# Shifting the stationary weight parts by 128 bytes in an fp32 decoder layer, and undividing the divided products

## The chip, the cores and the metric

One Trainium2 chip, one core. The metric is the device time of one execution of the kernel, in microseconds (us); the lower the better. TensorE (PE) multiplies; each of its products is a weight load (PEld: 128 columns of the operand that stands still, the stationary one) and a matmul that streams the other operand (the moving one) past it into PSUM. VectorE (DVE), ScalarE (ACT) and GpSimd (POOL) work element by element; SyncE (SP) issues the weight transfers.

## The reference

One decoder layer on 256 rows of width 2048, all in fp32:

```
h += 0.5 * post_norm(FFN1(rms_norm(h)))            SwiGLU, d_ff 5632
h += post_norm([conv_group ; moba_group] @ w_out)  one input projection, 5 x 1024 columns
h += post_norm(attn(rms_norm(h), rms_norm(mem)) @ w_o)   cross-attention, 4 heads, 256 memory rows
h += 0.5 * post_norm(FFN2(rms_norm(h)))
```

With 256 rows in one block, the block-sparse attention is plain causal attention with 8 heads of 128. The convolution has 31 taps and 1024 channels, and is followed by a layer norm and a swish.

## The kernel before, in words

**Products in three parts.** Every large product is made of TensorE products of type fp32r. Weights and activations are split into a high part (hi, an ACT copy) and a low part (lo, the rest, a DVE subtraction), and x times w is made as hi*hi + lo*hi + hi*lo: three products of 256 moving columns each, which write to the same place in PSUM.

**The weight stream (class `Weights`).** The weights arrive as entries of 128 x 1024 numbers in the order of use: SP loads an entry into one of 4 `raw` tiles, ACT writes its hi part into one of 4 `hi` tiles (L199 with a gain, L197 without), DVE its lo part into one of 3 `lo` tiles (L215, L213). `step` (L341) calls `W.ahead()`, which queues splits up to three entries ahead for hi and two for lo, then issues the 24 products of one entry, then one step of the background queue `bg`. Some entries are split early and kept in the general 8 KB buffers called `ck` (chunk): the activations, and of the weights those of the cross-attention's keys and of its output projection.

**Which operand stands still.** In `proj_T` (L485: both gate-up stages, the input projection's groups other than v, the cross-attention's q) the weight part is stationary and the activations' chunk moves. In `proj` (L499: both down stages, v, the two output projections) a chunk is stationary and the weight part moves. Each entry is 24 products: 16 with hi, 8 with lo. One gate-up is 22 groups of 8 entries (4,224 products), one down 88 entries (2,112).

**Where the tiles stand.** SBUF addresses are counted in bytes within a partition. In the program as built, the `hi` and `lo` tiles are 4096 bytes each and all start at 64 modulo 256; the chunks are 8192 bytes each and all start at 128 modulo 256. All slices that a product reads start a multiple of 512 bytes into their tile. Below, **the offset** of a product is the address of its stationary slice less that of its moving slice, modulo 256: 192 in the gate-ups and the input projection (64 - 128), 64 in the downs and in v (128 - 64), and 0 where chunk meets chunk, which is so in the cross-attention's keys (L485, `ps<-ck`) and its output projection (L499, `ps<-ck`).

**Divided products.** `HALVED = (0, 4, 8)` names three of the products of one entry (or of one half of it) which are issued as two matmuls of 128 columns instead of one of 256. That is done at 15 places, once each: in the first gate-up at (group, entry) (0, 2) and (3, 1); in the second at (1, 1) and (2, 1); in each of the three downs at entry 1 and entry 5 of the first column half; in groups 1 and 3 of the gated convolution and in the second group of q and k; and in both v groups.

**Interruptions.** Between these products TensorE makes small plain fp32 products, each of them two passes (two loads and two matmuls): the row-scale product at L447, `ones` times a diagonal, which spreads the rows' scales over the lanes (five times: in both gate-ups, in the second half of the first down, in the input projection and in the cross-attention's q), the attention's scores and values, the layer norm's sums (L993, L1009) and transposes (L362, L398).

**The stretch before the second gate-up.** After the attention weights' values (`x_values`) the split heads `oT` are stationary in the output projection. Before it, `W.ahead(2, 2)`, and after its first half `W.ahead()`, let ACT and DVE split the first entries of the second gate-up. Then come the post norm, the residual, transposes and splits of the new rows (L370 hi, L373 lo), and the gate-up starts.

Of the kernel before, what the change touches and what calls it, by code (L numbers as in the profile page):

```python
# [26 lines left out]
SCALE = 128.0 ** -0.5  # L27
RAW, HI, LO, TMP = 4, 4, 3, 4
STEP_DVE, STEP_ACT, STEP_POOL = 1.2, 1.3, 2.4
# [5 lines left out]
SIDE = 3  # L35
HALVED = (0, 4, 8)
MEM_AT = [20, 22, 24, 26]
# [63 lines left out]
class Weights:  # L101


    def __init__(self, nc, pool, chunk, sm):
        self.nc, self.pool, self.chunk, self.sm = nc, pool, chunk, sm
        self.entries = []
        self.raw, self.hi, self.lo, self.chunks = {}, {}, {}, {}
        self.n_raw = self.n_hi = self.n_lo = self.pos = 0
        self.marks = []
        self.limit = None  # L110

    def add(self, src, gains=(None,), key=None, rows=False):
        self.entries.append((src, gains, key, rows))

    def load(self, upto):
# [6 lines left out]
    def start(self):  # L122
# [12 lines left out]
        self.hi[key], self.lo[key] = ck[:, :, 0, :], ck[:, :, 1, :]  # L135
        self.hi[1] = self.pool.tile([P, 1024], F32R, name="hi", bufs=HI)
        self.lo[1] = self.pool.tile([P, 1024], F32R, name="lo", bufs=LO)

# [42 lines left out]
    def split_hi(self, upto):  # L181
        while self.n_hi < min(upto + 1, len(self.entries)):
            i = self.n_hi
            self.load(i)
            _, _, key, rows = self.entries[i]
            if rows:
                self.chunks[key] = c = self.chunk()
                self.hi[key], self.lo[key] = c[:, :, 0, :], c[:, :, 1, :]
            elif key is not None:
                c = self.chunk().rearrange("p a b c -> p (a b c)")  # L190
                self.hi[key], self.lo[key] = c[:, 0:1024], c[:, 1024:2048]
            else:
                key = i
                self.hi[key] = self.pool.tile([P, 1024], F32R, name="hi", bufs=HI)
            for src, dst, g in self.parts(i, self.hi[key]):
                if g is None:
                    self.nc.scalar.activation(dst, src, AF.Copy)  # L197
                else:
                    self.nc.scalar.activation(dst, src, AF.Copy, scale=g)  # L199
            self.n_hi += 1  # L200

    def split_lo(self, upto):
        while self.n_lo < min(upto + 1, len(self.entries)):
# [3 lines left out]
            if key is None:  # L207
                key = i
                self.lo[key] = self.pool.tile([P, 1024], F32R, name="lo", bufs=LO)
            his = self.parts(i, self.hi[key])  # L210
# [33 lines left out]
def layer_kernel(ctx: ExitStack, tc: tile.TileContext, x, mem, eye, consts, smalls, post_g, xt, memt,  # L244
# [51 lines left out]
    def add_ffn(gu, down, gain, extra, side):  # L296
        for n, (g, u) in enumerate(gu_order(side)):
            extra(-1, n)
            W.add(gu[g, u], [gain + 2 * u, gain + 2 * u + 1])
        for hf in range(2):  # L300
# [20 lines left out]
    for n in range(10):  # L321
        for u in range(8):
            W.add(w_in[n, u])
    for hf in range(2):
# [5 lines left out]
    for n in range(16):  # L330
        u = n % 8
        if n < 8:
            W.add(x_q[u], [S_GX + 2 * u, S_GX + 2 * u + 1])
        else:
            W.add(x_v[u // 4, u % 4])
# [153 lines left out]
    def proj(pss, first, last, hi, lo, xk, t, n0=0, halved=(), sides=(0, 256)):  # L489

        xs = [xk[:, f, t * P:(t + 1) * P] for f in (0, 1, 0)]
        m = 0
# [62 lines left out]

    def down(nk, lhs, post, hook=None, tail=TAIL, keep=False, order=None):

        order = order or range(nk)
        for hf in range(2):
# [3 lines left out]
            def mm(n, hi, lo):  # L563
# [3 lines left out]
                for t in range(2):  # L567
                    at = HALVED if t == 0 and (hf, n) in ((0, 1), (0, 5)) else ()
                    proj(pss[t], n == 0, n == nk - 1, hi, lo, lhs(order[n]), t, 0, at)
# [218 lines left out]
    post = Post(0, 4.0)  # L788
    last = down(KF, lambda k: hT[k // 4][:, k % 4], post, ffn1_hook)

# [61 lines left out]
    def glu_group(q):  # L852
        pss = in_group(halved=HALVED if q % 2 else ())
        box = []
# [222 lines left out]
    def v_group(c, hook):  # L1077
# [3 lines left out]
        def mm(u, hi, lo):  # L1081
            for e in range(2):
                k = 2 * u + e
                for t in range(2):
                    at = [m - 6 * t for m in HALVED] if u == 2 and e == 0 else ()
                    proj([vps[t]], k == 0, k == KT - 1, hi[:, e * 512:], lo[:, e * 512:], rows.x(k), t, 0, at)

# [14 lines left out]
    for c in range(2):  # L1102
        for p in range(2):
            pss = in_group(lambda u: norm_conv(c == 1 and p == 1 and u == 5), HALVED if (c, p) == (0, 1) else ())
            if p == 0:
# [99 lines left out]
    warm_sqrt()  # L1205
    oT = chunk()
    post = Post(2, 1.0)

    def x_values(hh):
        o_ = bank()  # L1210
        for t in range(2):
            nc.tensor.matmul(o_[:, :256], vx[:, hh // 2, t, (hh % 2) * P:(hh % 2 + 1) * P],  # L1212
                             pxT[:, hh * 512 + t * 256:hh * 512 + (t + 1) * 256], start=t == 0, stop=t == 1)
        make_hi(oT[:, hh, 0, :], o_[:, :256])
        make_lo(oT[:, hh, 1, :], o_[:, :256], oT[:, hh, 0, :])

    for hh in range(XH):
        x_values(hh)
    W.ahead(2, 2)
    wo = [W.held(("o", u)) for u in range(8)]  # L1220
    ps0 = [bank() for _ in range(4)]
    for hf in range(2):
        for k in range(XH):
            proj(ps0[2 * hf:2 * hf + 2], k == 0, k == XH - 1, *wo[4 * hf + k], oT[:, k], 0)
    W.ahead()
    rows = Rows(h_rows)
# [9 lines left out]
    for c in range(4):  # L1236
        ps1.append(bank())
        for sides in [(0, 256)] if c < 3 else [(0,), (256,)]:
            for k in range(XH):
                proj([ps1[c]], k == 0, k == XH - 1, *wo[4 * (c // 2) + k], oT[:, k], 1, c % 2, (), sides)  # L1240
    for c in range(4):
# [136 lines left out]
```

## Time and profile before

| | |
|---|---|
| median of 3 runs | 1901.75 us (1901.65 to 1904.34) |
| profiled execution | 1902.49 us, of which 1900.7 us span |
| TensorE busy | 1888.0 us, 99% of the span |
| TensorE's weight loads busy | 1883.2 us, 99% |
| VectorE, ScalarE, GpSimd busy | 62%, 55%, 11% |
| TensorE clock granted, mean | 0.999 of full |

TensorE is never idle for long, so the time is the number of products by the time from one product's start to the next one's, plus the short stops. A busy share of 99% says nothing about that pace; the starts of the weight loads do, and the rows below show them.

### The profile page before, as it was taken

The numbers are of one execution on the slowest core, as the hardware profiler recorded it, in microseconds if no ns is written. First come the engines' busy times: TensorE is split into PE (matmuls) and PEld (weight loads), VectorE is DVE, ScalarE is ACT, GpSimd is POOL, SyncE is SP. The second block draws the span as 40 slices with busy tenths as digits, with TensorE's granted clock in tenths as the row PEclk, the third lists the DMA queues.
The fourth block names the chain that finished last, engine by engine and source line by source line (L and its number), as shares of the span: only waits on it lengthen the run. The fifth ranks groups of instructions, "written<-read, shape, count | busy, mean of one in ns | idle before, by whom it ended". The sixth has DMA issues, their size and how long they took to land.

```text
span 1900.7 us, 39775 instructions
## 1 busy us (share of the span) xinstructions
PE 1888.0 (99%) x16445; PEld 1883.2 (99%) x16445; DVE 1179.5 (62%) x1615; ACT 1049.8 (55%) x1631; POOL 204.3 (11%) x182
## 2 busy tenths in 40 slices
PE   9999999999999999999999999999999999999998
PEld 9999999999999999999999999999999999999998
DVE  5666666666545556899885676666666666544444
ACT  6655555555434546687675565555555555433433
POOL 0000000000000000598510000000000000000000
PEclk9999999999999999999999999999999999999999
DMA  8555555555655675555555563565555555655554
GB/s 300 203 190 196 193 195 193 193 196 191 218 191 196 245 235 173 183 180 189 176 189 186 176 228 107 181 198 191 193 196 194 195 192 197 213 196 191 196 193 145
DMA packets 102278, 370.29 MB, mean 195 GB/s; under 512 B 11472, under 2 KB 11984, under 8 KB 101328
## 3 DMA queue, kind: packets, MB, share of 16 engines
q1 hardware_dynamic: 100944, 360.96, 56.0%
q10 hardware_dynamic: 1152, 6.79, 1.0%
q8 instruction: 128, 2.10, 0.4%
q14 instruction: 54, 0.44, 0.1%
HBM read 365.61 MB, written 2.10 MB: 193 GB/s over the span
## 4 chain that ended last, share of the span: by engine, by line
PE 95%; ACT 2%; DMA 1%; DVE 1%; issue 0%; SPq 0%; DVEq 0%; ACTq 0%
PE ps L485 60%; PE ps L499 34%; DMA raw<-in_x_v_dram 1%; ACT hi L199 0%; ACT tmp L367 0%; DMA raw<-in_xt_dram 0%; PE ps L362 0%; DMA raw<-in_f_gu_dram 0%; DVE lo L213 0%; PE ps L926 0%; PE ps L1212 0%; PE ps L955 0%; ACT hi L197 0%; ACT cf L725 0%; PE ps L942 0%
## 5 line engine op out<-in xcount | busy, mean ns | idle before, releaser
L485 PE MATMUL ps<-ck,hi 128*128 128x256 f32 x6798 | 1162.1, 277 | 2.7 <-ACT hi L199 1.0
L485 PEld LDWEIGHTS ps<-ck,hi 128*128 128x128 f32 x6798 | 1023.9, 188 | 4.3 <-ACT hi L199 1.2
L485 PE MATMUL ps<-ck,lo 128*128 128x256 f32 x3399 | 934.7, 276 | 0.1
L215 DVE SCALAR_TENSOR_TENSOR lo<-raw,sm,hi 128x512 fp32r<-128x512 f32 x718 | 517.5, 762 | 349.7 <-issue 328.5
L199 ACT ACTIVATE hi<-raw,sm 128x512 fp32r<-128x512 f32 x718 | 479.2, 716 | 363.3 <-PE ps L485 217.4
L485 PEld LDWEIGHTS ps<-ck,lo 128*128 128x128 f32 x3399 | 636.0, 188 | 0.3 <-DVE lo L215 0.3
L499 PE MATMUL ps<-hi,ck 128*128 128x256 f32 x3600 | 618.9, 277 | 0.0
L213 DVE TENSOR_TENSOR lo<-raw,hi 128x1024 fp32r<-128x1024 f32 x296 | 376.2, 1272 | 297.0 <-PE ps L499 231.5
L499 PEld LDWEIGHTS ps<-hi,ck 128*128 128x128 f32 x3600 | 544.0, 188 | 0.4
L499 PE MATMUL ps<-lo,ck 128*128 128x256 f32 (+1 forms) x1800 | 497.4, 277 | 0.0
L197 ACT ACTIVATE hi<-raw 128x1024 fp32r<-128x1024 f32 x296 | 312.7, 1059 | 318.9 <-PE ps L499 250.0
L499 PEld LDWEIGHTS ps<-lo,ck 128*128 128x128 f32 x1800 | 337.4, 188 | 0.2 <-DVE lo L213 0.2
L682 POOL TENSOR_TENSOR tmp<-tmp,rb 128x512 f32<-128x512 f32 x44 | 57.8, 1314 | 1125.4 <-ACT tmp L681 1125.4
L835 POOL TENSOR_TENSOR cv<-cv,cf 128x255 f32<-128x255 f32 (+14 forms) x120 | 123.4, 1029 | 307.8 <-ACT cf L834 299.5
L834 ACT ACTIVATE cf<-yv,cf 128x255 f32<-128x255 f32 (+14 forms) x120 | 56.6, 491 | 24.6 <-POOL cv L835 24.2
L825 DVE SCALAR_TENSOR_TENSOR ps<-yv,cf,ps 128x254 f32<-128x254 f32 (+28 forms) x116 | 54.4, 469 | 2.5
L370 ACT ACTIVATE ck<-tmp 128x512 fp32r<-128x512 f32 x44 | 27.8, 633 | 46.4 <-DVE tmp L685 46.4
L367 ACT ACTIVATE tmp<-ps 128x512 f32<-128x512 f32 (+1 forms) x33 | 19.3, 586 | 35.7 <-PE ps L499 31.2
L524 DVE TENSOR_TENSOR fg<-ps,cf 128x512 f32<-128x512 f32 x32 | 21.3, 684 | 15.9 <-ACT tmp L367 15.9
L678 DVE TENSOR_TENSOR tmp<-ps,rb 128x512 f32<-128x512 f32 x44 | 30.1, 683 | 0.1
L373 DVE TENSOR_TENSOR ck<-tmp,ck 128x512 fp32r<-128x512 f32 x44 | 30.1, 683 | 0.0
L685 DVE TENSOR_TENSOR tmp<-tmp,ps 128x512 f32<-128x512 f32 x44 | 29.7, 675 | 0.0
(137 smaller groups left out, 649.4 us busy)
## 6 DMA issues: line engine op xcount, KB each, us to landing
raw<-in_f_gu_dram SPq DMA_DIRECT2D x351, 512.0 KB, 3.4
raw<-in_f_down_dram SPq DMA_DIRECT2D x176, 512.0 KB, 4.2
raw<-in_w_in_dram SPq DMA_DIRECT2D x80, 512.0 KB, 3.3
raw<-in_w_out_dram SPq DMA_DIRECT2D x32, 512.0 KB, 3.3
cf<-in_post_g_dram ACTq DMA_DIRECT2D x4, 1024.0 KB, 7.0
raw<-in_x_k_dram SPq DMA_DIRECT2D x8, 512.0 KB, 4.4
raw<-in_x_q_dram SPq DMA_DIRECT2D x8, 512.0 KB, 3.8
raw<-in_x_o_dram SPq DMA_DIRECT2D x8, 512.0 KB, 3.6
```

Of the source, the lines that this page charges most:

```text
L197: self.nc.scalar.activation(dst, src, AF.Copy)
L199: self.nc.scalar.activation(dst, src, AF.Copy, scale=g)
L213: self.nc.vector.tensor_tensor(dst, src, hi.bitcast(F32), ALU.subtract)
L215: self.nc.vector.scalar_tensor_tensor(dst, src, g, hi.bitcast(F32), ALU.mult, ALU.subtract)
L373: nc.vector.tensor_tensor(lo, src, hi.bitcast(F32), ALU.subtract)
L485: nc.tensor.matmul(ps[:, o + a:o + a + w], (hi, hi, lo)[i][:, j * P:(j + 1) * P], xk[:, i % 2, a:a + w], start=first and o == 0 and i == 0 ...
L499: nc.tensor.matmul(ps[:, a:a + d], xs[i], w[:, c:c + d], start=first and a == 0 and i == 0, stop=last and i == 2, skip_group_check=True)
L678: nc.vector.tensor_tensor(two(box[0]), two(G), bc2(rows.rb), ALU.mult)
L682: nc.gpsimd.tensor_tensor(two(box[0]), two(box[0]), bc2(rows.rb), ALU.mult)
L825: nc.vector.scalar_tensor_tensor(o, yv[:, ct, :S - s], w, a[:, s:], ALU.mult, ALU.add)
L834: nc.scalar.activation(pr[:, :S - s], yv[:, ct, :S - s], AF.Copy, scale=w)
L835: nc.gpsimd.tensor_tensor(cv[:, ct, s:], cv[:, ct, s:], pr[:, :S - s], ALU.add)
```

## The change

Three things change. First, the `hi` and `lo` tiles are 4352 bytes (256 more), and where the weight part will be stationary it is written 128 bytes further back in its tile: the gate-ups, the input projection but for v (entries 6 and 9), and the cross-attention's q. To make room one of the four `tmp` buffers goes. Second, the heads `oT` of the cross-attention stand in one `hi` and one `lo` tile, shifted too, instead of in a chunk; the two `W.ahead` calls around the output projection go. Third, `HALVED` is empty, so that no product is divided anywhere (the places `again=(1, 20)` and `q == 1` have no effect with it).

In the program as built, the tiles start at 64 modulo 256 as before, so the shifted parts at 192, and the chunks at 128. The offset becomes 64 in the gate-ups, the input projection and q, stays 64 in the downs and v, becomes 64 in the output projection of the cross-attention, and stays 0 in its keys. As a tile is now 17 times 256 bytes, neighbouring tiles differ by 256 modulo 512.

```diff
-RAW, HI, LO, TMP = 4, 4, 3, 4
+RAW, HI, LO, TMP = 4, 4, 3, 3
+SHIFT = 32
...
-HALVED = (0, 4, 8)
+HALVED = ()
...
+    def part_tile(self, name, shift):
+
+        t = self.pool.tile([P, 1024 + 64], F32R, name=name, bufs={"hi": HI, "lo": LO}[name])
+        return t[:, shift:shift + 1024]
...
-                self.hi[key] = self.pool.tile([P, 1024], F32R, name="hi", bufs=HI)
+                self.hi[key] = self.part_tile("hi", self.shifts[i])
...
-                self.lo[key] = self.pool.tile([P, 1024], F32R, name="lo", bufs=LO)
+                self.lo[key] = self.part_tile("lo", self.shifts[i])
...
-            W.add(gu[g, u], [gain + 2 * u, gain + 2 * u + 1])
+            W.add(gu[g, u], [gain + 2 * u, gain + 2 * u + 1], shift=SHIFT)
...
-            W.add(w_in[n, u])
+            W.add(w_in[n, u], shift=0 if n in (6, 9) else SHIFT)
...
-            W.add(x_q[u], [S_GX + 2 * u, S_GX + 2 * u + 1])
+            W.add(x_q[u], [S_GX + 2 * u, S_GX + 2 * u + 1], shift=SHIFT)
...
-                    at = HALVED if t == 0 and (hf, n) in ((0, 1), (0, 5)) else ()
+                    at = HALVED if t == 0 and (hf, n) in ((0, 1), again) else ()
...
-    oT = chunk()
+    oT = [W.part_tile(name, SHIFT).rearrange("p (k s) -> p k s", k=XH) for name in ("hi", "lo")]
...
-        make_hi(oT[:, hh, 0, :], o_[:, :256])
-        make_lo(oT[:, hh, 1, :], o_[:, :256], oT[:, hh, 0, :])
+        make_hi(oT[0][:, hh], o_[:, :256])
+        make_lo(oT[1][:, hh], o_[:, :256], oT[0][:, hh])
...
-    W.ahead(2, 2)
...
-    W.ahead()
```

The first place is on TensorE in the first gate-up, entry 2 of group 0, the first of the 15 divided places (`ck` is the moving chunk, `hi` and `lo` the stationary parts). Before:

```order
L485 MATMUL ps<-ck,hi 128x128 x2
L485 MATMUL ps<-ck,hi 128x256
L485 MATMUL ps<-ck,lo 128x256
L485 MATMUL ps<-ck,hi 128x256
L485 MATMUL ps<-ck,hi 128x128 x2
L485 MATMUL ps<-ck,lo 128x256
L485 MATMUL ps<-ck,hi 128x256 x2
L485 MATMUL ps<-ck,lo 128x128 x2
```

Now:

```order
L493 MATMUL ps<-ck,hi 128x256 x2
L493 MATMUL ps<-ck,lo 128x256
L493 MATMUL ps<-ck,hi 128x256 x2
L493 MATMUL ps<-ck,lo 128x256
L493 MATMUL ps<-ck,hi 128x256 x2
L493 MATMUL ps<-ck,lo 128x256
```

Three products that were two matmuls of 128 columns are one of 256 each; nothing else moves there.

The second place is on DVE, from the heads' low parts (before at L373 into `ck`, now at L381 into `lo`) over the post norm (L524 to L553 before) to the first entries of the second gate-up (L215 before, L223 now). Before:

```order
L373 TENSOR_TENSOR ck<-ps,ck 128x256 x4
L215 SCALAR_TENSOR_TENSOR lo<-raw,sm,hi 128x512 x4
L524 TENSOR_TENSOR fg<-ps,cf 128x512 x3
```

and further on, ahead of the second entry's products:

```order
L373 TENSOR_TENSOR ck<-ps,ck 128x4x128
L524 TENSOR_TENSOR fg<-ps,cf 128x512
L215 SCALAR_TENSOR_TENSOR lo<-raw,sm,hi 128x512 x4
L373 TENSOR_TENSOR ck<-ps,ck 128x4x128
```

Now, the same two pieces:

```order
L381 TENSOR_TENSOR lo<-ps,hi 128x256 x4
L535 TENSOR_TENSOR fg<-ps,cf 128x512 x3
```

```order
L381 TENSOR_TENSOR ck<-ps,ck 128x4x128
L535 TENSOR_TENSOR fg<-ps,cf 128x512
L223 SCALAR_TENSOR_TENSOR lo<-raw,sm,hi 128x512 x8
L381 TENSOR_TENSOR ck<-ps,ck 128x4x128
```

Four low halves (two entries) that stood ahead of the post norm stand behind it, in one row of eight ahead of the row block's low part (L373 before, L381 now). On ACT the high halves move in the same way: four that stood ahead of the post norm's squares are now in a row of eight behind the row blocks' high parts. On SP and POOL the order is the same.

## Rows read from the trace of the kernel before

**Rows 1.** The page of the profile: span, clock granted by slice, shares of the last chain.
```profile
span 1900.7 us, 39775 instructions
...
PEclk9999999999999999999999999999999999999999
...
PE 95%; ACT 2%; DMA 1%; DVE 1%; issue 0%; SPq 0%; DVEq 0%; ACTq 0%
```

**Rows 2.** Stretches of time (us), weight loads alone: length, busy us (count), clock, DMA.
```profile
82.00:482.00 400.00, 400.00 (x3531) 1.00 0.58 194
500.00:650.00 150.00, 150.00 (x1325) 1.00 0.60 208
664.00:728.00 64.00, 64.00 (x545) 1.00 0.75 246
780.00:870.00 90.00, 90.00 (x795) 1.00 0.54 185
1200.00:1648.00 448.00, 448.00 (x3955) 1.00 0.57 194
1660.00:1880.00 220.00, 220.00 (x1942) 1.00 0.57 192
```

**Rows 3.** Weight loads in order of time around 62 us: start us, us, instruction, count.
```profile
62.35 0.30 PEld L447 LDWEIGHTS ps<-tmp,ones 128*128 128x128 f32 x2
62.68 0.41 PEld L485 LDWEIGHTS ps<-ck,hi 128*128 128x128 f32 x2
63.01 0.19 PEld L485 LDWEIGHTS ps<-ck,lo 128*128 128x128 f32 x1
...
76.44 0.19 PEld L485 LDWEIGHTS ps<-ck,lo 128*128 128x128 f32 x1
```

**Rows 4.** Groups by line and shape, the output projection: count, busy us, mean ns, idle.
```profile
L499 PEld LDWEIGHTS ps<-ck 128*128 128x128 f32 x192 | 23.2, 192 | 0.1
```

**Rows 5.** Weight loads in order of time, a divided place of the input projection.
```profile
815.74 0.19 PEld L485 LDWEIGHTS ps<-ck,lo 128*128 128x128 f32 x1
815.85 0.41 PEld L485 LDWEIGHTS ps<-ck,hi 128*128 128x128 f32 x3
...
817.43 0.19 PEld L485 LDWEIGHTS ps<-ck,lo 128*128 128x128 f32 x1
```

**Rows 6.** Weight loads in order of time, first gate-up into first down product.
```profile
487.88 0.19 PEld L485 LDWEIGHTS ps<-ck,lo 128*128 128x128 f32 x1
...
488.22 0.19 PEld L499 LDWEIGHTS ps<-lo,ck 128*128 128x128 f32 x1
...
488.58 0.19 PEld L499 LDWEIGHTS ps<-lo,ck 128*128 128x128 f32 x1
...
488.93 0.19 PEld L499 LDWEIGHTS ps<-lo,ck 128*128 128x128 f32 x1
```

**Rows 7.** Weight loads in order of time after the row-scale product at 660 us.
```profile
660.55 0.40 PEld L499 LDWEIGHTS ps<-hi,ck 128*128 128x128 f32 x2
...
661.24 0.19 PEld L499 LDWEIGHTS ps<-lo,ck 128*128 128x128 f32 x1
...
661.60 0.19 PEld L499 LDWEIGHTS ps<-lo,ck 128*128 128x128 f32 x1
```

**Rows 8.** Weight loads in order of time after the layer norm sums at 954 us.
```profile
954.52 0.41 PEld L499 LDWEIGHTS ps<-hi,ck 128*128 128x128 f32 x2
...
955.21 0.19 PEld L499 LDWEIGHTS ps<-lo,ck 128*128 128x128 f32 x1
...
955.55 0.19 PEld L499 LDWEIGHTS ps<-lo,ck 128*128 128x128 f32 x1
```

**Rows 9.** Weight loads in order of time, row-scale product before the second gate-up.
```profile
1193.39 0.30 PEld L447 LDWEIGHTS ps<-tmp,ones 128*128 128x128 f32 x2
1193.72 0.41 PEld L485 LDWEIGHTS ps<-ck,hi 128*128 128x128 f32 x2
```

**Rows 10.** All engines in order of time, output projection and start of second gate-up.
```profile
1143.10 2.73 DVE L215 SCALAR_TENSOR_TENSOR lo<-raw,sm,hi 128x512 fp32r<-128x512 f32 x4
...
1168.69 1.00 PEld L485 LDWEIGHTS ps<-ck,hi 128*128 128x128 f32 x8 [0.71 <-ACT ck L370]
...
1171.74 2.73 DVE L215 SCALAR_TENSOR_TENSOR lo<-raw,sm,hi 128x512 fp32r<-128x512 f32 x4
...
1174.39 0.68 DVE L373 TENSOR_TENSOR ck<-ps,ck 128x512 fp32r<-128x512 f32 x1
...
1175.12 0.19 PEld L485 LDWEIGHTS ps<-ck,hi 128*128 128x128 f32 x1 [0.17 <-DVE ck L373]
```

More of the change, by code (lines that the diff above doesn't have):

```diff
@@ L106, in __init__ @@
         self.entries = []
+        self.shifts = []
         self.raw, self.hi, self.lo, self.chunks = {}, {}, {}, {}
@@ L110, in __init__, with add @@
         self.limit = None
-    def add(self, src, gains=(None,), key=None, rows=False):
+    def add(self, src, gains=(None,), key=None, rows=False, shift=0):
         self.entries.append((src, gains, key, rows))
+        self.shifts.append(shift)
+    def part_tile(self, name, shift):
+        t = self.pool.tile([P, 1024 + 64], F32R, name=name, bufs={"hi": HI, "lo": LO}[name])
+        return t[:, shift:shift + 1024]
     def load(self, upto):
@@ L135, in start @@
         self.hi[key], self.lo[key] = ck[:, :, 0, :], ck[:, :, 1, :]
-        self.hi[1] = self.pool.tile([P, 1024], F32R, name="hi", bufs=HI)
-        self.lo[1] = self.pool.tile([P, 1024], F32R, name="lo", bufs=LO)
+        self.hi[1] = self.part_tile("hi", self.shifts[1])
+        self.lo[1] = self.part_tile("lo", self.shifts[1])
         def split(i, c, k):
@@ L489, in proj @@
     def proj(pss, first, last, hi, lo, xk, t, n0=0, halved=(), sides=(0, 256)):
-        xs = [xk[:, f, t * P:(t + 1) * P] for f in (0, 1, 0)]
+        if isinstance(xk, tuple):
+            xs = [xk[f][:, t * P:(t + 1) * P] for f in (0, 1, 0)]
+        else:
+            xs = [xk[:, f, t * P:(t + 1) * P] for f in (0, 1, 0)]
         m = 0
@@ L554, in update, with down @@
                                            ALU.mult, ALU.add)
-    def down(nk, lhs, post, hook=None, tail=TAIL, keep=False, order=None):
+    def down(nk, lhs, post, hook=None, tail=TAIL, keep=False, order=None, again=None):
         order = order or range(nk)
@@ L788, in layer_kernel @@
     post = Post(0, 4.0)
-    last = down(KF, lambda k: hT[k // 4][:, k % 4], post, ffn1_hook)
+    last = down(KF, lambda k: hT[k // 4][:, k % 4], post, ffn1_hook, again=(1, 20))
     rows = Rows(h_rows, gain=S_GM)
@@ L852, in glu_group @@
     def glu_group(q):
-        pss = in_group(halved=HALVED if q % 2 else ())
+        pss = in_group(halved=HALVED if q == 1 else ())
         box = []
@@ L1084, in mm @@
                 for t in range(2):
-                    at = [m - 6 * t for m in HALVED] if u == 2 and e == 0 else ()
-                    proj([vps[t]], k == 0, k == KT - 1, hi[:, e * 512:], lo[:, e * 512:], rows.x(k), t, 0, at)
+                    proj([vps[t]], k == 0, k == KT - 1, hi[:, e * 512:], lo[:, e * 512:], rows.x(k), t)
         for u in range(8):
@@ L1103, in layer_kernel @@
         for p in range(2):
-            pss = in_group(lambda u: norm_conv(c == 1 and p == 1 and u == 5), HALVED if (c, p) == (0, 1) else ())
+            pss = in_group(lambda u: norm_conv(c == 1 and p == 1 and u == 5))
             if p == 0:
@@ L1223, in layer_kernel @@
         for k in range(XH):
-            proj(ps0[2 * hf:2 * hf + 2], k == 0, k == XH - 1, *wo[4 * hf + k], oT[:, k], 0)
-    W.ahead()
+            proj(ps0[2 * hf:2 * hf + 2], k == 0, k == XH - 1, *wo[4 * hf + k], (oT[0][:, k], oT[1][:, k]), 0)
     rows = Rows(h_rows)
@@ L1239, in layer_kernel @@
             for k in range(XH):
-                proj([ps1[c]], k == 0, k == XH - 1, *wo[4 * (c // 2) + k], oT[:, k], 1, c % 2, (), sides)
+                proj([ps1[c]], k == 0, k == XH - 1, *wo[4 * (c // 2) + k], (oT[0][:, k], oT[1][:, k]), 1, c % 2, (), sides)
     for c in range(4):
```

## Prediction

> **What bounds the kernel now.** I read the page first: the span is 1900.7 us, the granted clock is at full speed (2.4 GHz) in every slice, and the chain that ended last is 95% TensorE [rows 1]. So the time is a number of products times a pace, and a few stops. The busy share can't show the pace, since a weight load's row is longer than the distance to the next load; the number of loads in a long undisturbed stretch can. There [rows 2] shows two levels. 3,531 loads in 400 us are 113.3 ns each (82 to 482 us); the stretches at 500, 780, 1200 and 1660 us give 113.2 to 113.3. The stretch at 664 us is different: 545 loads in 64 us are 117.4 ns. The second level is seen more exactly in the first gate-up, right behind the row-scale product L447: from 63.01 to 76.44 us stand 114 products, 13.43 / 114 = 117.8 ns [rows 3]. A third level is the output projection of the cross-attention, whose 192 loads take 23.2 us, 120.8 ns with its stops [rows 4].
>
> Call 113.3 fast and 117.8 slow. The same line (L485 in gate-ups, L499 in downs) shows both at a full clock, so the products' type and shape do not decide. Each interruption of the stream sets the pace, and the next one keeps or changes it. I went through all interruptions in the loads' order:
> - Behind each of the divided places in the gate-ups, the downs and the gated convolution the stream goes on fast, whatever it was before. In the first gate-up the slow stretch of rows 3 ends at such a place.
> - At the boundary from gate-up into down the pace turns slow: three products took 488.22 - 487.88 = 0.34 us before it, 0.36 and 0.35 behind it [rows 6], until the divided place of entry 1. The same holds at 1652, at 879 (into v) and at 1111 us.
> - Behind L447 it is slow at offset 192 all four times; two of them begin with the same pair of loads of 0.41 us [rows 3, 9]. At offset 64 there is one case, in the first down, and it is slow too: the pair takes 0.40, three products 0.36 [rows 7], and the pace stays slow for the stretch at 664 us.
> - Behind other pauses of small fp32 products it is fast 13 times of 17 at offset 64 (one of them: 955.55 - 955.21 = 0.34, [rows 8], though the pair is 0.41 there), 9 times of 26 at offset 192.
>
> So offset 64 makes the fast pace likelier but doesn't force it, and offset 0 is the worst. The divided places are what forces it.
>
> **The change, part by part.** The profiled execution took 1902.49 us, 0.74 above the median; sums are made on its time and 0.74 is taken off at the end.
>
> *The undivided products themselves.* At a divided place four threes of products and three more pieces take 817.43 - 815.74 = 1.69 us [rows 5]; twelve products at 113.3 ns are 1.36. A place thus costs 0.33 us, and 15 places give back **-5.0 us**. Bounds: 0.28 against slow neighbours (12 at 117.8 are 1.41) to 0.42, that is -4.2 to -6.
>
> *What the divided places kept fast.* Going slow costs 4.45 ns a product. By the counts of [rows 2]: first gate-up 3,531, **15.7 us**; first down up to L447, 1,325, **5.9**; gated convolution 795, **3.5**; second gate-up 3,955, **17.6**; second down 1,942, **8.6**. The windows leave off some us at the ends of each stretch. I estimate what these add at 1.2 us for the downs and the convolution and 0.5 for each gate-up, by 3.9% (4.45 / 113.3) of some 30 and 12 us left off.
>
> Which of these go slow? The downs had offset 64 before and have it now, and the boundary into them is still an offset-0 crossing (a chunk's load follows a chunk's stream), slow 4 times of 4. Nothing but the divided place ended that. So I take both downs slow. In the input projection the stretch at 780 us starts behind L447 at 766 us; I take it slow too, with less confidence since its interruptions are several. Together 5.9 + 8.6 + 3.5 + 1.2 = **+19.2 us**.
>
> For the gate-ups the offset does change, from 192 to 64. Each is entered through L447, which is slow 1 of 1 at 64 [rows 7], where other pauses are mostly fast [rows 8]. The start of both gate-ups with its hi and lo halves in separate tiles resembles neither fully. I judge it slightly more likely that the new offset keeps them fast: then they cost nothing, and the 118 slow products behind L447 [rows 3] become fast, **-0.5 us**. The other bound is +34.3 (15.7 + 17.6 + 1.0).
>
> *The shorter background.* `W.ahead` gone: four low halves (2.73 us, 1143.10) lay in idle time of DVE under the output projection. Now they join the row at 1171.74, ahead of the row block's low part at 1174.39, for which TensorE waits (its load at 1175.12 shows L373 as the releaser) [rows 10]. Nothing hides them there: the low part comes 2.73 us later and so do the products behind it, **+2.7 us**. Behind the waiting load stand the rest of the gate-up's steps, so the stop is not made up. Bounds: 0.7, if products of the rows before fill the wait, to 4.1, if ACT's four high halves (1.3 for two) come into the same chain.
>
> *The heads' tiles.* The output projection goes from offset 0 to 64: 191 products at 6 ns less (120.8 to about 114.5) are **-1.2 us**; -0.4 if it is slow. Its stationary parts are now held in one `hi` and one `lo` tile, so the entries ahead have one tile less; what waits for that is the splits already priced.
>
> *One `tmp` buffer less, larger tiles.* The orders of SP and POOL are unchanged and DVE is 62% busy, ACT 55%; the transfers ask at most 0.75 of the DMA engines [rows 2]. I price it at nothing; a post norm that waits for a buffer once per row block would cost up to 1 us.
>
> Sum: 1902.49 - 5.0 + 19.2 - 0.5 + 2.7 - 1.2 = 1917.7, less 0.74: **1917 us**.
>
> **Trainium skill.** The page TensorE: Matmul & The Clock Gate (Step-by-step: what each phase is for) says that TensorE has two independent SBUF read ports, so that loading the next weights does not take read bandwidth from the running matmul. By that rule the place of an operand can't matter, and this change gives its divided pieces back and nothing else; that is the last of the rivals below. The trace disagrees as far as it goes: chunk against chunk runs at 120.8 ns [rows 4], others at 113.3 and 117.8 [rows 2, 3].
>
> **Rivals.**
> - *Both gate-ups slow as well.* For: L447 at offset 64 was slow [rows 7]. Against: 13 of 17 other restarts. 1917 + 34.3 + 0.5 = **1952**.
> - *One gate-up slow*: the two are entered alike, yet the second starts with a stop and other tiles. 1917 + 17 = **1934**.
> - *A down or the gated convolution stays fast*, because their next interruption (a pause, not a division) turns the pace: 1917 less 4 to 9, **1908 to 1913**; two of them, about 1903.
> - *Fast everywhere (the other side).* The slow pace at offset 64 is a leftover of what ran at 192 or 0 before it: when nearly all products stand at 64, there is nothing to turn the stream slow. For: stalls inside offset 64 restart fast. Against: the boundaries 4 of 4, and rows 7, where the stream had been at 64 for 170 us. It decides as soon as more than 19.2 of the slow us fail to come, for the sum without them is 1902.49 - 5.0 - 0.5 + 2.7 - 1.2 - 2.4 (545 products of the stretch at 664 us, 4.45 ns each) - 0.74 = **1895**.
> - *The place has no effect, nor have the divisions*: each stretch keeps its present pace and the pieces are saved. 1902.49 - 5.0 + 2.7 - 0.74 = **1899.5**. Against it stands the turn at divided places.
>
> **Numbers.** 1917: 0.33; 1952: 0.24; 1934: 0.13; 1908 to 1913: 0.11; 1895: 0.14; 1899.5: 0.05. A change within 0.2% (1898 to 1905.5) can't be told from none here. Faster: the 0.14 and 0.02 of the last, 0.16. The same: the rest of it and the case of two that stay fast, 0.09. Slower: 0.75. The range is 1897 to 1953: it leaves out the fast rival and the upper part of the case at 1952. The likeliest alone, with its bounds (-1 to +1.4 for the pieces and the wait, 0.8 for the heads, 1 for the buffer, 3.5 for the convolution), is 1911 to 1921.
>
> **What would show it.** Loads in a 400 us window of the first gate-up: 3,531 if fast, about 3,396 if slow; the same for the second. In the downs 1,274 in place of 1,325 per 150 us. A MATMUL's mean row in a gate-up tells it too. Threes of loads behind 488 and 1652 us: 0.353 throughout, not 0.34 from entry 1 on. The output projection: 192 loads in about 22 us. At the second gate-up's start a DVE row of eight low halves, then L381 some 2.7 us after the heads' rows would put it, and TensorE waiting for it. The prediction is wrong if the downs show 0.34 without a divided place, if the gate-ups change pace in their middle where nothing interrupts them, or if the granted clock falls below full anywhere, at the longer stop in front of the second gate-up above all: none of the prices holds such a fall.

## The result and the profile after

The changed kernel takes 1919.97 us in the median of 6 runs (1918.06 to 1932.45), the kernel before 1902.43 us in its 6 (1901.65 to 1904.34): ratio 1.0107, interval 1.0085 to 1.0129. It is slower by about 1%. The runs of the changed kernel are wider apart than those of before: four lie at 1918 to 1920, two at 1928 and 1932. The profiled execution is one of the four; its span is 1918.5 us, 17.8 more than before.

The page of the profile after (span, shares of the last chain) says only that TensorE is still what ends last:

```profile
span 1918.5 us, 39692 instructions
...
PE 98%; DMA 1%; DVE 1%; ACT 0%; issue 0%; SPq 0%; DVEq 0%; ACTq 0%
```

The counts of weight loads by stretch are what answers to [rows 2]. The columns: stretch, its length, busy us (number of loads), granted clock, DMA share, GB/s.

```profile
82.00:482.00 400.00, 400.00 (x3531) 1.00 0.60 194
500.00:650.00 150.00, 150.00 (x1275) 1.00 0.60 201
664.00:728.00 64.00, 63.95 (x543) 1.00 0.73 245
780.00:870.00 90.00, 90.00 (x766) 1.00 0.57 187
1225.00:1665.00 440.00, 440.00 (x3883) 1.00 0.59 195
1675.00:1895.00 220.00, 220.00 (x1870) 1.00 0.57 187
```

The first gate-up has the same 3,531 loads in 400 us as before, with nothing divided in it, and the second has 3,883 in 440 us, 113.3 ns each. The first down has 1,275 in 150 us in place of 1,325 (117.6 ns), the gated convolution 766 in 90 in place of 795, the second down 1,870 in 220 in place of 1,942. The stretch at 664 us is as slow as before. So the gate-ups are fast from their row-scale products on, the downs and the convolution slow. The beginning of the first gate-up is not fast in the changed kernel:

```profile
22.00:60.00 38.00, 38.00 (x324) 1.00 0.86 294
```

That is 117.3 ns a product, where the kernel before has 337 loads in the same window, three of them pieces of its divided place.

Weight loads in order of time, behind the first row-scale product (now L455) and at the boundary into the first down (L510), which answer to [rows 3, 6]:

```profile
63.57 0.41 PEld L493 LDWEIGHTS ps<-ck,hi 128*128 128x128 f32 x2
...
487.68 0.30 PEld L493 LDWEIGHTS ps<-ck,hi 128*128 128x128 f32 x2
...
488.02 0.30 PEld L510 LDWEIGHTS ps<-hi,ck 128*128 128x128 f32 x2
...
488.37 0.31 PEld L510 LDWEIGHTS ps<-hi,ck 128*128 128x128 f32 x2
...
488.73 0.31 PEld L510 LDWEIGHTS ps<-hi,ck 128*128 128x128 f32 x2
```

Behind the row-scale product the same pair of 0.41 us stands as in [rows 3], and yet a fast stretch follows it. At the boundary three products take 488.02 - 487.68 = 0.34 us before it and 0.35 and 0.36 behind it, and now nothing ends that: it lasts to the row-scale product in the down, and the stretch at 664 us behind it is slow too.

The start of the second gate-up, all engines in order of time, answers to [rows 10]:

```profile
1173.96 0.99 PEld L493 LDWEIGHTS ps<-ck,hi 128*128 128x128 f32 x8 [0.71 <-ACT ck L378]
...
1177.02 4.05 DVE L223 SCALAR_TENSOR_TENSOR lo<-raw,sm,hi 128x512 fp32r<-128x512 f32 x6
...
1177.82 0.93 PEld L493 LDWEIGHTS ps<-ck,lo 128*128 128x128 f32 x4 [2.86 <-DVE lo L223]
```

TensorE's products with the low part (1177.82) wait 2.86 us for the first of the DVE halves that were no longer split ahead; DVE, busy with the row blocks' low parts and the post norm (L381, L564, L535), comes to it at 1177.02. Behind this stop the granted clock shows what the prediction had no price for (the same columns as above, TensorE's matmuls):

```profile
1170.00:1174.00 4.00, 3.07 (x26) 1.00 0.00 0
...
1177.80:1179.00 1.20, 1.18 (x5) 0.50 0.00 0
...
1182.00:1183.00 1.00, 1.00 (x7) 0.50 0.89 287
```

From 1177.8 to 1183 us the grant is 0.50, the lower level (1.2 GHz), after 1.00 before the stop.

The output projection is the last reading: its first and last loads,

```profile
1148.39 0.19 PEld L510 LDWEIGHTS ps<-ck,hi 128*128 128x128 f32 x1
...
1170.15 0.19 PEld L510 LDWEIGHTS ps<-ck,hi 128*128 128x128 f32 x1
```

are 21.76 us apart over 191 steps, 113.9 ns with its stops, where [rows 4] gave 120.8.

The 17.8 us, stretch by stretch, from the starts of the same products in both traces:

| stretch | before, us | after, us | difference |
|---|---|---|---|
| start to the first row-scale product | 62.35 | 63.24 | +0.89 |
| from there to the first down | 425.64 | 424.78 | -0.86 |
| first down to the row-scale product in it | 172.24 | 178.08 | +5.84 |
| from there to the input projection's row-scale product | 105.66 | 105.70 | +0.04 |
| from there to v (gated convolution) | 113.20 | 116.33 | +3.13 |
| v, q and k, attention, output projection, to the row-scale product in the cross-attention's q | 228.32 | 225.90 | -2.42 |
| from there to the cross-attention's output projection | 34.51 | 34.36 | -0.15 |
| that output projection to the second gate-up | 26.77 | 25.57 | -1.20 |
| second gate-up to its row-scale product | 24.70 | 29.82 | +5.12 |
| from there to the second down | 458.20 | 457.42 | -0.78 |
| second down to the end | 249.11 | 257.30 | +8.19 |

### The profile page after: what moved, and what is told of

It is laid out like the page before. It is cut to its first block, busy times and chain, and to the rows that moved or that the text cites. A ratio compares the mean times of both kernels' runs of the same rounds, so it can differ in the third digit from the quotient of the medians.

```text
span 1918.5 us, 39692 instructions
## 1 busy us (share of the span) xinstructions
PE 1903.3 (99%) x16400; PEld 1899.0 (99%) x16400; DVE 1179.5 (61%) x1615; ACT 1049.8 (55%) x1631; POOL 202.8 (11%) x182
## 4 chain that ended last, share of the span: by engine, by line
PE 98%; DMA 1%; DVE 1%; ACT 0%; issue 0%; SPq 0%; DVEq 0%; ACTq 0%
PE ps L493 61%; PE ps L510 34%; PE ps L370 0%; PE ps L1202 0%; DMA raw<-in_xt_dram 0%; DMA raw<-in_f_gu_dram 0%; PE ps L1201 0%; PE ps L1200 0%; PE ps L937 0%; PE ps L1222 0%; PE ps L1160 0%; PE ps L966 0%; DVE ck L381 0%; ACT tmp L375 0%; ACT hi L207 0%
## 5 line engine op out<-in xcount | busy, mean ns | idle before, releaser
L223 DVE SCALAR_TENSOR_TENSOR lo<-raw,sm,hi 128x512 fp32r<-128x512 f32 x718 | 517.1, 762 | 351.9 <-issue 327.6
L510 PE MATMUL ps<-hi,ck 128*128 128x256 f32 x3584 | 631.4, 281 | 0.0
L510 PEld LDWEIGHTS ps<-hi,ck 128*128 128x128 f32 x3584 | 548.9, 189 | 0.4
L510 PE MATMUL ps<-lo,ck 128*128 128x256 f32 x1792 | 502.0, 280 | 0.0
L510 PEld LDWEIGHTS ps<-lo,ck 128*128 128x128 f32 x1792 | 336.4, 188 | 0.0
L535 DVE TENSOR_TENSOR fg<-ps,cf 128x512 f32<-128x512 f32 x32 | 21.3, 684 | 17.5 <-ACT tmp L375 17.5
L381 DVE TENSOR_TENSOR ck<-tmp,ck 128x512 fp32r<-128x512 f32 x44 | 30.0, 683 | 0.0
```

The lines of the kernel that those rows point to most:

```text
L223: self.nc.vector.scalar_tensor_tensor(dst, src, g, hi.bitcast(F32), ALU.mult, ALU.subtract)
L381: nc.vector.tensor_tensor(lo, src, hi.bitcast(F32), ALU.subtract)
L510: nc.tensor.matmul(ps[:, a:a + d], xs[i], w[:, c:c + d], start=first and a == 0 and i == 0, stop=last and i == 2, skip_group_check=True)
```

## The experiments

Eleven runs, each beside runs of the kernel before on the same chip (medians 1902.19 to 1902.72 us).

| run | median, us | lowest to highest | ratio, interval |
|---|---|---|---|
| changed, downs divided | 1912.95 | 1902.74 to 1922.62 (10 runs) | 1.0054, 1.0023 to 1.0085 |
| before, nothing divided | 1952.20 | 1951.97 to 1952.47 (4) | 1.0262, 1.0244 to 1.0279 |
| changed, shift 0 | 1957.29 | 1956.62 to 1958.09 (4) | 1.0289, 1.0274 to 1.0304 |
| changed, splits ahead | 1920.45 | 1914.52 to 1934.78 (4) | 1.0106, 1.0062 to 1.0150 |
| changed, nine places divided, splits ahead | 1899.54 | 1897.48 to 1916.79 (12) | 0.9990, 0.9975 to 1.0006 |
| that, downs undivided, chunk-by-chunk product | 1919.15 | 1918.67 to 1919.63 (2) | 1.0085, 1.0068 to 1.0103 |
| the same, ordinary product | 1922.36 | 1917.82 to 1926.90 (2) | 1.0102, 1.0083 to 1.0122 |
| nine places, one product divided | 1896.45 | 1895.00 to 1897.62 (4) | 0.9966, 0.9953 to 0.9979 |
| changed, shift 192 bytes | 1962.14 | 1950.92 to 1962.90 (3) | 1.0295, 1.0264 to 1.0327 |
| changed, shift 64 bytes | 1963.76 | 1962.86 to 1964.02 (3) | 1.0321, 1.0304 to 1.0338 |
| before, one product divided | 1937.44 | 1935.84 to 1938.22 (4) | 1.0183, 1.0168 to 1.0198 |

**Downs divided.**

```diff
-at = HALVED if t == 0 and (hf, n) in ((0, 1), again) else ()
+at = (0, 4, 8) if t == 0 and (hf, n) in ((0, 1), again) else ()
```

> The changed kernel with divided products in the downs alone: at entry 1 of each of the three downs, and in the first down also right behind the row-scale product in its second half. Theory A (the pace is a state that a boundary or a pause sets and a divided place sets to fast): the 150 us window of the first down goes from 1,275 loads back to 1,325, the second down's 220 us window from 1,870 to about 1,942, the stretch behind the row-scale product too becomes fast; in time -5.9 -2.6 -8.6 -0.8 for the ends +1.3 for four places, about 1903 us from 1920. Rival B (the downs are slow in the changed kernel because of the larger tiles, whose neighbours differ by 256 modulo 512, or because of the lost buffer): the windows stay at 1,275 and 1,870 and the time becomes 1921.

The ten runs fall into two groups of five, 1902.7 to 1905.5 and 1920.4 to 1922.6. The profiled execution belongs to the second. Its loads by stretch:

```profile
500.00:650.00 150.00, 150.00 (x1325) 1.00 0.61 209
670.00:720.00 50.00, 50.00 (x443) 1.00 0.75 252
1220.00:1660.00 440.00, 440.00 (x3737) 1.00 0.56 187
1690.00:1900.00 210.00, 210.00 (x1854) 1.00 0.58 191
```

The downs are fast again (1,325 in 150 us, 1,854 in 210, and the stretch behind the row-scale product 443 in 50). In the first down both divided places turn the pace: 117.8 ns a product ahead of each, 113.3 behind. Theory A holds there, the larger tiles have no part in it. The second down shows nothing of the kind, since it is fast from the boundary on, ahead of its divided place. And the second gate-up, which no division touches, is slow here: 3,737 in 440 us are 117.7 ns. The five short runs are 18 us shorter, about what this stretch costs; no trace of one was taken.

**Nothing divided in the kernel before.**

```diff
-HALVED = (0, 4, 8)
+HALVED = ()
```

> The kernel before, with all 15 divided places undivided and nothing else changed: weight parts unshifted, offset 192 in the gate-ups. Theory A: both gate-ups, which are entered through the row-scale product and were slow behind it at this offset all four times, go slow to their ends (400 us hold about 3,396 loads), and the downs and the gated convolution too: 1902 - 5.0 + 16.2 + 18.0 + 5.9 + 8.6 + 3.5 + 1.2 = about 1951 us. Rival C (the offset has nothing to do with it, the gate-ups are fast by themselves and only the downs and the convolution need the divided places): gate-ups keep 3,531 loads in 400 us, time about 1916.

```profile
82.00:482.00 400.00, 400.00 (x3397) 1.00 0.57 187
520.00:670.00 150.00, 150.00 (x1275) 1.00 0.60 201
1230.00:1680.00 450.00, 450.00 (x3822) 1.00 0.57 187
```

Theory A's 1951 against 1952.2 measured: both gate-ups and the first down are slow here (3,397 in 400 us, 1,275 in 150, 3,822 in 450), and the second down (1,700 loads from 1700 to 1900 us) as well; all four runs lie within 0.5 us. Without its divided places the kernel before loses 50 us.

**A shift of 0.**

```diff
-SHIFT = 32
+SHIFT = 0
```

> The changed kernel with a shift of 0: tiles of the same larger size, everything else as changed, but the weight parts stand where they stood before (offset 192 in gate-ups, input projection, q and the cross-attention's output projection). Theory A (the 128 bytes are what keeps the gate-ups fast): both gate-ups slow, 1920 + 16 + 18 = about 1953 us, and 3,396 loads in 400 us. Rival D (what keeps them fast is the larger tile, so that neighbouring tiles no longer lie alike, or the missing splits ahead): gate-ups stay at 3,531, time about 1920.

```profile
82.00:482.00 400.00, 400.00 (x3398) 1.00 0.57 187
...
1230.00:1680.00 450.00, 450.00 (x3822) 1.00 0.56 187
```

1957.3 us, and all four runs lie within 1.5 us; in the trace both gate-ups are slow. The 128 bytes, and neither the tile size nor the lost buffer, are what lets the changed kernel's gate-ups be fast. The Trainium skill's page TensorE: Matmul & The Clock Gate (Step-by-step: what each phase is for) says that loading the next weights takes no SBUF read bandwidth from the running matmul. Read as the prediction reads it, that would leave no difference between this run and the changed kernel; they are 37 us apart.

**Splits ahead.**

```diff
     for hh in range(XH):
         x_values(hh)
+    W.ahead(2, 1)
```

> The changed kernel with splits of the second gate-up's first entries put back ahead of the cross-attention's output projection (three high parts and two low parts, the most that the tiles hold beside the heads). Theory A: the stop of 2.9 us on the low parts at the second gate-up's start goes, and the fall of the granted clock to half in the 5 us behind it as well; about 4.9 us less, 1915, clock full throughout, paces elsewhere unchanged. Rival E (the stop comes from the post norm's chain with one buffer less, or the fall of the clock comes from something else): the stop and the fall stay, time 1919 to 1920.

The loads by stretch of the profiled execution (span 1933.0), and the wait for a DVE half that is left at the start of the second gate-up:

```profile
82.00:482.00 400.00, 400.00 (x3397) 1.00 0.57 187
510.00:660.00 150.00, 150.00 (x1325) 1.00 0.62 207
1220.00:1660.00 440.00, 440.00 (x3737) 1.00 0.57 187
1700.00:1900.00 200.00, 200.00 (x1767) 1.00 0.59 193
```

```profile
1187.11 0.19 PEld L493 LDWEIGHTS ps<-ck,lo 128*128 128x128 f32 x1 [0.28 <-DVE lo L223]
```

From the second gate-up's first product to its row-scale product it is now 26.16 us instead of 29.82, and the grant is 1.00 throughout: 3.7 of the 5.1 us come back, less than expected, since waits of 0.28 us for a half and 1.21 us for a chunk's low part (L381) stay. The median of the four runs shows none of it (1920.45 us), because their paces differ. That settles the cause of the stop; the fall of the clock goes with it. The loads show something else. Here both gate-ups are slow (3,397 and 3,737) and, with no division anywhere, both downs are fast (1,325, and 1,767 in 200). Slow before the boundary, fast behind it; fast before it in the changed kernel's trace, slow behind it. The boundary does not make the pace slow. It changes it.

**Nine places divided, splits ahead.**

```diff
-HALVED = ()
+HALVED = (0, 4, 8)
...
+    W.ahead(2, 1)
```

> The changed kernel with divided products back at nine places (two in each gate-up, entry 1 of each down, one behind the row-scale product in the first down, one in the gated convolution) and with the splits ahead of the output projection. Theory A, by which the gate-ups' pace at offset 64 is not certain in each execution and a divided place makes it so: every execution has both gate-ups fast, so the spread of the runs falls from some 20 us to about 2 us, and the time is 1903.3 (the short runs of the kernel with divided downs) - 3.6 for the splits - 3.9 for the convolution - 1.6 for the first gate-up's beginning + 1.7 for five places more = about 1896 us. Rival F (the spread comes from elsewhere, the transfers or the clock): it stays at 10 to 20 us.

Eleven of twelve runs lie at 1897.5 to 1901.0, one at 1916.8. The spread is mostly gone, as theory A has it, but not wholly, and the time is 3.5 us above the expected one. In the profiled execution (span 1897.4) seven of the eight places in the gate-ups, the two FFN downs and the convolution are followed by the fast pace (five of them were slow ahead), and one, the first in the second gate-up, is not; the next place mends it. Three divided products do not always do it at offset 64.

**A chunk-by-chunk product.** The kernel of the last run with the downs undivided, and this:

```diff
+if u == 0 and g == 11 and side > 1:
+    nc.tensor.matmul(pss[g][0][:, :256], rows.x(0)[:, 0, :P], rows.x(0)[:, 0, :256],
+                     start=True, stop=True, skip_group_check=True)
```

> As the kernel with nine divided places and splits ahead, but with no division in the downs, and with one added product at the start of group 11 of the first gate-up, in which a chunk is stationary and the same chunk moves (its result is overwritten by the next product). Its load meets a moving chunk at offset 0, once, as at the boundary into a down. Theory G (such a crossing turns the pace into the other one, fast to slow and slow to fast): the first gate-up is fast up to about 275 us and slow from there to the boundary (window 300 to 470: 1,443 loads instead of 1,501), and the first down is fast without a division (1,325 loads in 150 us), the second slow (1,870 in 220); time 1896 + 9.4 + 2.6 + 9.0 - 1.3 = about 1916. Rival H (the boundary makes the pace slow whatever it was, by the change of the moving tile): gate-up fast throughout or slow from there, but both downs slow; 1912 or 1922.

Loads around the added product (L714), then by stretch (the first window lies ahead of the first row-scale product):

```profile
248.47 0.30 PEld L493 LDWEIGHTS ps<-ck,hi 128*128 128x128 f32 x2
...
248.81 0.19 PEld L714 LDWEIGHTS ps<-ck 128*128 128x128 f32 x1
248.92 0.31 PEld L493 LDWEIGHTS ps<-ck,hi 128*128 128x128 f32 x2
...
249.28 0.31 PEld L493 LDWEIGHTS ps<-ck,hi 128*128 128x128 f32 x2
```

```profile
40.00:62.00 22.00, 22.00 (x196) 1.00 0.73 245
...
90.00:240.00 150.00, 150.00 (x1325) 1.00 0.58 194
260.00:490.00 230.00, 230.00 (x1954) 1.00 0.57 187
510.00:660.00 150.00, 150.00 (x1326) 1.00 0.61 208
1240.00:1665.00 425.00, 425.00 (x3749) 1.00 0.59 197
1680.00:1880.00 200.00, 200.00 (x1700) 1.00 0.57 186
```

Three products take 0.34 us up to the added one and 0.36 behind it; the gate-up goes on slow for 230 us (1,954, 117.7 ns), the boundary into the down turns it back to fast (1,326 in 150 us), and the second gate-up, fast to its end, turns to slow (1,700 in 200). In this trace one load at offset 0 was enough. Theory G holds; 1919 measured, 1916 expected. Not tested apart is whether the offset of this load did it, or that a chunk was stationary for one product.

**An ordinary product** at the same place, `hi[:, :P]` in place of the stationary chunk.

> The control to the kernel with the added chunk-by-chunk product: the added product at the same place has the weight part as its stationary operand, offset 64 like its neighbours; no division in the downs. Theory G: nothing turns, the first gate-up is fast to its end (1,501 loads from 300 to 470 us), both downs are slow (1,275 in 150, 1,870 in 220); 1896 + 6.3 + 2.6 + 9.0 - 1.3 = about 1912 us. Rival I (any added product turns the pace): slow from group 11 on and the first down fast, 1916.

```profile
40.00:62.00 22.00, 22.00 (x189) 1.00 0.77 248
...
82.00:482.00 400.00, 400.00 (x3397) 1.00 0.57 187
...
510.00:660.00 150.00, 150.00 (x1325) 1.00 0.63 208
1240.00:1665.00 425.00, 425.00 (x3752) 1.00 0.59 194
1690.00:1890.00 200.00, 200.00 (x1700) 1.00 0.56 187
```

As a control it says this much: the first gate-up has one pace throughout (3,397 in 400 us), so nothing turns at the added product. That pace is the slow one, though two divided places of three products each stand ahead of it, and then the boundary gives a fast first down (1,325). The second boundary goes from fast to slow. The expected times are not met for that reason. Rival I falls for a slow stream; whether an ordinary product turns a fast one, no trace shows.

**One product divided** at each of the nine places.

```diff
-HALVED = (0, 4, 8)
+HALVED = (0,)
```

> As the kernel with nine divided places and splits ahead, but with one product instead of three divided at each place. If one division is enough to make the pace fast: the same windows as there and 9 places x two pieces x 0.11 = 2 us less, about 1894 us. Rival (one division only adds a step that may turn the pace or leave it, three are needed): some of the stretches are slow, each for its price of 3.5 to 18 us; 1900 to 1940 us, with a spread of more than 5 us.

```profile
82.00:482.00 400.00, 400.00 (x3531) 1.00 0.60 194
500.00:650.00 150.00, 150.00 (x1325) 1.00 0.61 208
...
1200.00:1648.00 448.00, 448.00 (x3954) 1.00 0.60 195
1660.00:1880.00 220.00, 220.00 (x1943) 1.00 0.56 187
```

All nine places are followed by the fast pace; six of them found a slow stretch and turned it, three a fast one. The four runs lie within 2.6 us. At 1896.45 us this version beats both kernels, by 0.34% the one before.

**Other shifts**, `SHIFT = 48` and `SHIFT = 16` (192 and 64 bytes) in the changed kernel.

> The changed kernel with the weight parts 192 bytes back in their tiles instead of 128: the offset in the gate-ups, the input projection and q becomes 128 (and in the cross-attention's output projection), everything else as changed, nothing divided. Theory J (what counts is how far the two operands are apart modulo 256, so 128 is the best): the gate-ups are fast in every execution, the spread of some 14 us goes, 1918 us; the downs stay slow. Rival K (the two paces belong to any offset but 0, and which one comes is settled at the pauses): one or both gate-ups slow in some executions, 1918 to 1953, with a spread.

> The changed kernel with the weight parts 64 bytes back: offset 0 in the gate-ups, the input projection, q and the cross-attention's output projection, everything else as changed. If the offset alone makes the third pace (120 ns, seen only where chunk meets chunk): 8,448 products of the gate-ups at 6.7 ns more, 56.6 us, and some 1,700 of the input projection and q at 2.2 to 6.7, about 5, so about 1980 us, with next to no spread, and 400 us hold about 3,333 loads. If the third pace belongs to chunks and not to the offset: 1918 to 1955 us.

The first, and then the second:

```profile
82.00:482.00 400.00, 400.00 (x3335) 1.00 0.56 184
```

```profile
82.00:482.00 400.00, 400.00 (x3335) 1.00 0.56 183
520.00:670.00 150.00, 150.00 (x1325) 1.00 0.61 205
```

Offset 128 is worse than 64 and as bad as 0 in the first gate-up: 3,335 loads in 400 us, 119.9 ns. In the second gate-up of the same trace it is 118.6 (3,878 in 460 us). Both J and K are wrong. One of the three runs at 128 is 11 to 12 us shorter than the others (1950.92 us); no trace of it was taken. Offset 0 gives the same 119.9 with a moving chunk and a stationary weight part, so the third pace belongs to the offset and not to chunks. The expected 1980 for it was too high, because behind these gate-ups the downs came out fast (1,325 in the first, 1,590 in 180 us in the second), some 15 us that I had counted as slow.

**One product divided in the kernel before.**

> The kernel before with one product instead of three divided at each of its 15 places (offset 192 in the gate-ups, no shift). If one division makes the pace fast at either offset: 15 places x 2 pieces x 0.11 = 3.3 us less, about 1899 us. If at offset 192 one division is not enough: gate-ups or the convolution slow, 1905 to 1940 us.

```profile
90.00:490.00 400.00, 400.00 (x3398) 1.00 0.57 187
520.00:670.00 150.00, 150.00 (x1325) 1.00 0.64 208
```

At offset 192 one division does not do it: behind all seven places in the gate-ups and the input projection ahead of v the pace is slow (3,398 in 400 us). The downs of this trace, at offset 64, are fast, but they are so from the boundary on, ahead of their divided places (in the first, 18 products from 506.35 to 508.39 us, 113.3 ns each), and show nothing of a division. Beside the nine places at offset 64 with one product divided, what a single division does depends on the offset.

## Why the prediction was right, and where it was not

The forecast of 1917 us with fast gate-ups, slow downs and a slow convolution is what the profiled execution shows stretch by stretch; four of the six runs lie within 4 us of it. In part that is luck: the fast gate-ups (the whole case had been given a chance of 0.33) are one outcome of several that the same kernel has, and two steps of the reasoning were wrong where the number came out.

- **The undivided products** (-5.0). The stretch from the row-scale product to the first down loses 0.86 us: one place at 0.33 and the 118 products of [rows 3] at 4.45 ns, 0.53. The stretch from v to the cross-attention's q holds four places (1.3) and loses 2.4, with other small changes of pace in it. The first is as priced; in the second the pieces can't be told apart from the rest.
- **What the divided places kept fast** (+19.2, pieces not counted). First down +5.8, convolution +3.1, second down +8.2, together 17.2 with the pieces of seven places (2.3) given back in them: 19.5 went into the slower pace. The size is right. For the first down the run with divided downs shows the cause: its places turn slow into fast.
- **The reason given for it failed.** I wrote that at the boundary the pace turns slow and that nothing but the divided place ended that. At offset 64 the boundary turns fast into slow and slow into fast: 14 of 14 gate-ups in the seven traces with the 128 bytes, among them five from slow to fast. The boundary into v does so too, 7 times of 7. One load at offset 0 does the same inside a gate-up. In the trace of before I had seen only fast gate-ups, and so only one half of it. At offset 192 it is not as regular: slow gate-ups stayed slow into the down in the undivided kernel before and with a shift of 0, and turned fast in the kernel before with one division.
- **Divided places "force" the fast pace.** At 192 the seven places of three divisions in the trace of before are all followed by the fast pace (three of them were slow ahead), those of one division never (7 of 7 slow). At 64 three failed at three places in two traces; one was followed by the fast pace at nine of nine.
- **The gate-ups' rivals were no rivals.** I gave the cases of one or two slow gate-ups chances as if one of them would be the kernel's. They are executions of the same kernel, as the two groups with divided downs suggest: what follows the row-scale product at offset 64 differs from trace to trace, fast in the changed kernel's, slow in that with the splits ahead, one of each in that with divided downs. I also took the row-scale product for what sets the gate-up's pace, from its one case in the first down. In the gate-ups at offset 64 it leaves the pace as it was, 13 times of 14 (the chunk-by-chunk run has 196 loads in 22 us ahead of it and is fast behind, its control 189 and slow behind); the exception is the first gate-up of the changed kernel's trace, slow ahead and fast behind. At offset 192 the pace behind it is slow 8 times of 8, in three of them out of a fast one. So at 64 the gate-up's pace is mostly decided before it, in the opening products. And the rivals' price is smaller than I gave, since a slow gate-up brings a fast down: about 16 - 6 in the first pair and 18 - 9 in the second, some 9 or 10 us, where I had 17. The run at 1928.5 is about where one such pair would put it, the one at 1932.5 some 3 us above; no trace of them was taken.
- **The splits ahead** (+2.7, bounds 0.7 to 4.1) cost 5.1. The stop itself was 2.86, near the 2.73 of the four halves, but it is another wait: not for the row block's low part behind a row of eight halves, but for the first half itself, to which DVE came only at 1177.02. That the two lengths agree is luck. The rest comes with the clock at half for 5 us behind the stop. The prediction named such a fall as a sign of being wrong and had no price for it.
- **The heads' tiles** (-1.2): -1.2. **The smaller `tmp`** (0): no wait on it was found among the releasers of TensorE's stops.
- The first stretch is 0.9 us longer, for which the sum has no term. TensorE's first products start at 6.78 instead of 5.57 us, because ACT waits longer for the first weight transfer. In the traces of the eleven experiments they start at 5.39 to 6.33, so this need not belong to the change. From 22 to 60 us the slow pace holds back ten products, some 1.2 us; a faster beginning ahead of 22 us takes that back, and 0.3 us more.

## What to carry to other kernels

A busy share of 99% can hide a 4 to 6% difference in pace: count the weight loads in long windows and compare stretches of the same line. Where stationary and moving operands stand relative to each other in SBUF is part of a kernel's tuning (128 bytes were worth 37 us here), and a gain seen in one trace may be one outcome of several, so look at the spread of the runs before and after. And work moved out of idle time to the start of a TensorE stage cost a stop of 2.86 us here, plus some 2 us that the clock lost behind it.

## What was not expected of the hardware

At a full granted clock 256-column fp32r products ran at three paces: 113.3, 117.7 and 119.9 ns. At an offset of 64 bytes (modulo 256) between stationary and moving operand 113.3 or 117.7, whichever an interruption left; at 192 the same two; at 0, and at 128 in the first gate-up, 119.9 (at 128 in the second, 118.6). The pace then stayed for more than 3,800 products (3,883 in 440 us). A single load at offset 0 in a stream at 64 exchanged the two paces in one trace, the boundary into a down or into v 21 times of 21. What sets the pace in a gate-up's opening products, why one divided product at 64 works where three sometimes fail, and why 192 behaves otherwise, stays open.
